# Masked products on GpSimd become block copies and column scalings in a gated delta mixer; all attention gates run on VectorE

## The chip, the cores and the metric

The kernel runs on one core of one Trainium2 chip. The metric is the device time of one execution in microseconds. A core has a matrix engine (TensorE, PE in the rows), and three engines for elementwise work: VectorE (DVE), ScalarE (ACT) and GpSimd (POOL). SyncE (SP) issues most DMAs. Each engine runs its own queue of instructions in order, and waits on semaphores for the others.

## The reference

Two model blocks are computed one after the other on 512 tokens of width 1024, all in float32. The first has two attention layers, worked in four units each; the change touches the gates of their outputs:

```python
def _merge(a_att, b_att, a_z, b_z, g_a, g_b, w_o_a, w_o_b, w_out):
    o_a = (a_att * jax.nn.silu(a_z)) @ w_o_a
    o_b = (b_att * jax.nn.silu(b_z)) @ w_o_b
    ...
```

The second block has two layers with feed-forward parts, a mixer and cross attention each. The second layer's mixer is a gated delta rule with 8 heads of width 128, in chunks of 128 tokens (4 chunks):

```python
    kkt = jnp.einsum('bhnid,bhnjd->bhnij', kb, k) * decay
    amat = jnp.eye(C, dtype=jnp.float32) + jnp.where(strict, kkt, 0.0)
    ...
    sol = lax.linalg.triangular_solve(amat, rhs, left_side=True, lower=True, unit_diagonal=True)
    ...
    def step(state, inp):
        q_i, k_i, u_i, w_i, qk_i, g_i = inp
        v_new = u_i - jnp.einsum('bhcd,bhde->bhce', w_i, state)
        o = (jnp.einsum('bhcd,bhde->bhce', q_i * jnp.exp(g_i)[..., None], state)
             + jnp.einsum('bhij,bhje->bhie', qk_i, v_new))
        ...
```

`q` and `k` are normalized by their length, `q`, `k` and `v` come from a causal convolution of four taps and a SiLU, and the result `o` is normalized over a head's columns, weighted, and multiplied with SiLU of a gate `z`.

## The kernel before

Matrix products with weights are done as three products of split operands: each weight tile `ws` is split into `wh` (ScalarE, line 114) and `wl` (VectorE, line 115), each activation into a high and a low part (`nh`, `nl` or `hh`, `hl`), and TensorE multiplies high by high, low by high and high by low (lines 131 to 133). Weights come in tiles of 512 KB by SP's queue.

In the attention layers, `gate` (line 897) multiplies a unit's finished output `o` (from L526) with the silu `z` and sends it to DRAM. There are four units in a layer; `o` has 1536 columns in the first layer and 1024 in the second. The last unit's gate (u = 3) is on VectorE, the others are on GpSimd. Around them the next unit's rotary products (L461 to L464, GpSimd), splits `hl` (L471, VectorE) and casts `qA`, `kA` (L479, VectorE) run for TensorE's transposes (L478) and scores (L493, L494).

The mixer `mixer1` (line 1733) goes through its 8 heads as a pipeline in rounds of some 41 us, one head's products entering while older heads are finished. In a head:

- `head` projects `k`, `q`, `z` and `v`, with the convolution steps `xc` (L1248, VectorE, four taps over 512 columns) and SiLUs (`kT`, `qT`, `vT`, L1488 and L1489). `e` holds the decays (L1522, L1525). `key` multiplies `e` by `rk`, the key lengths (L1543, GpSimd). `product` and `scaled` make `U` from the key products, `e` and a scale (L1550, L1554, VectorE).
- `solve` sends the 32 x 32 diagonal blocks of U to DRAM (`ud`) and fetches their 16 x 16 blocks as `D`. GpSimd inverts these by 15 steps of two instructions each, `T` (L1605) and `Y` (L1607), on 32 partitions. `Y` goes out as `yd` and back as `soC`.
- `inverse` spreads `soC` into the block-diagonal `X` (L1626, GpSimd, a product of a broadcast `soC` with the mask in `lev`). TensorE transposes X (L1635). At levels 4 and 5, GpSimd clears `W` (L1643) and makes `B`, U masked to the off-diagonal blocks of that level (L1644, a product with another mask in `lev`), which TensorE multiplies (L1648). VectorE corrects X and `Z` (L1655, L1656).
- `steps` runs the four chunks: TensorE multiplies the state (L1684, L1685), VectorE makes `R`, the new state and `o` (L1687, L1701, L1707). Then `o` is scaled by its columns of `orq` (L1722, GpSimd), and `finish` transposes it for the output (L1727, L1729).

`lev` is one tile of 128 x 384: two masks for the levels and the mask of the 16 x 16 diagonal blocks, fetched at the start of the mixer.

TensorE's order is written out by hand, by generators that yield. The other engines' instructions, and SP's DMAs, are ordered by the builder, which runs a timeline of its own and lets each engine take what is ready there first. A change of one instruction can so move others in the queues of VectorE, GpSimd and SP.

Of the kernel before, what the change touches and what calls it, by code (L numbers as in the profile page):

```python
# [8 lines left out]
F32 = mybir.dt.float32  # L9
# [3 lines left out]
OP = mybir.AluOpType  # L13
AX = mybir.AxisListType

P = 128
D = 1024
NCH = 8
S = 512
# [348 lines left out]
class Block1:  # L368
# [528 lines left out]
    def gate(self, l, u, o, z):  # L897

        n = (NT if l == 0 else 4) * 256
        eng = self.net.nc.vector if u == 3 else self.net.nc.gpsimd  # L900
        eng.tensor_tensor(out=o[:, :n], in0=o[:, :n], in1=z[:, :n], op=OP.mult)
        self.net.nc.sync.dma_start(self.units(self.od, l, u), o[:, :n])

    def early_gate(self, l, j):
# [208 lines left out]
class Block2:  # L1113
# [323 lines left out]
    def decays(self, pool):  # L1437

        net, nc, I = self.net, self.net.nc, self.net.I
        out = {}  # L1440
        yield from self.proj(I["dn_ab"], out, "p1", 16)
        yield
        ab = pool.tile([P, S], F32, name="ab", tag="dnB", bufs=1)[:16, :]
        nc.vector.tensor_tensor(ab, out["ps"], self.rb[:16, :], op=OP.mult)
        pt = net.psum("p3")
        for t in range(4):
            nc.tensor.transpose(pt[:, t * 16:(t + 1) * 16], ab[:, t * P:(t + 1) * P], net.ident[:16, :16])
        t3 = lambda name: pool.tile([P, 4, 8], F32, name=name, tag=f"dc{name}", bufs=1)
        v = pt[:, :64].rearrange("p (t a) -> p t a", a=16)
        dt = net.bcast_row(I["dn_dt_bias_2"][0], 8, "dtb", pool)  # L1450
        al = net.bcast_row(I["dn_a_log_2"][0], 8, "alog", pool)
        beta, x, gc = t3("beta"), t3("x"), t3("gc")
        nc.scalar.activation(beta, v[:, :, 8:16], AF.Tanh, scale=0.5)
        nc.vector.tensor_scalar(beta, beta, 0.5, 0.5, op0=OP.mult, op1=OP.add)
        nc.vector.tensor_tensor(x, v[:, :, 0:8], dt.unsqueeze(1).to_broadcast([P, 4, 8]), op=OP.add)
        sp = self.softplus(x.rearrange("p t h -> p (t h)"), 32, pool)
        nc.scalar.activation(al, al, AF.Exp)
        nc.vector.scalar_tensor_tensor(x, sp.rearrange("p (t h) -> p t h", h=8), -1.0,
                                       al.unsqueeze(1).to_broadcast([P, 4, 8]), op0=OP.mult, op1=OP.mult)
        yield  # L1460
        pg = net.psum("p3")
        g2 = x.rearrange("p t h -> p (t h)")
        nc.tensor.matmul(pg[:, 0:32], net.c["triu"], g2, start=True, stop=True)
        nc.tensor.matmul(pg[:, 32:64], net.c["ones"], g2, start=True, stop=True)
        nc.vector.tensor_copy(gc, pg[:, 0:32].rearrange("p (t h) -> p t h", h=8))
        gl = pg[:, 32:64].rearrange("p (t h) -> p t h", h=8)
        ngc, egc, egl, dk = t3("ngc"), t3("egc"), t3("egl"), t3("dk")
        nc.vector.tensor_scalar(ngc, gc, -1.0, None, op0=OP.mult)
        nc.scalar.activation(egc, gc, AF.Exp)
        nc.scalar.activation(egl, gl, AF.Exp)  # L1470
        nc.vector.tensor_tensor(dk, gl, gc, op=OP.subtract)
        nc.scalar.activation(dk, dk, AF.Exp)
        self.dc = dict(beta=beta, gc=gc, ngc=ngc, egc=egc, egl=egl, dk=dk)
        yield
# [16 lines left out]
    def head(self, h, hd, pool, late):  # L1491

        net, nc, I = self.net, self.net.nc, self.net.I
        cw = self.cw
        q4 = lambda a: a.rearrange("p (t d) -> p t d", d=P)
        bc = lambda a: a.unsqueeze(2).to_broadcast([P, 4, P])
        tl = lambda name, bufs: pool.tile([P, S], F32, name=name, tag=f"dn{name}", bufs=bufs)
# [6 lines left out]
        cols = lambda a: lambda t: a[:, t * P:(t + 1) * P]  # L1504
# [9 lines left out]
        dc, e, U, A = {}, tl("e", 1), tl("U", 2), tl("A", 3)  # L1514
# [21 lines left out]
        def key():  # L1536
            rk = st["k"]
            for n in ("b", "s", "w"):
                st[n] = small("n" + n)
            nc.vector.tensor_tensor(st["b"], rk, dc["beta"], op=OP.mult)  # L1540
            nc.vector.tensor_tensor(st["s"], rk, dc["dk"], op=OP.mult)
            nc.vector.scalar_tensor_tensor(st["w"], st["b"], -1.0, dc["egc"], op0=OP.mult, op1=OP.mult)
            nc.gpsimd.tensor_tensor(out=q4(e), in0=q4(e), in1=bc(rk), op=OP.mult)  # L1543

        def product(m, n):
            ps = net.psum("p3")
# [10 lines left out]
        z = tl("z", 3)  # L1557
# [58 lines left out]
    def inverse(self, hd, pool, wait):  # L1616

        net, nc = self.net, self.net.nc
        mm = nc.tensor.matmul
        q4 = lambda a: a.rearrange("p (t d) -> p t d", d=P)  # L1620
        tl = lambda name, bufs: pool.tile([P, S], F32, name=name, tag=f"dn{name}", bufs=bufs)
        lev = lambda l: self.lev[:, (l - 4) * P:(l - 3) * P].unsqueeze(1).to_broadcast([P, 4, P])
        U = hd["U"]
        hd["X"] = X = tl("X", 2)
        blocks = [P, 4, 8, 16]
        nc.gpsimd.tensor_tensor(out=X.rearrange("p (t m b) -> p t m b", t=4, b=16),  # L1626
                                in0=hd["blocks"].unsqueeze(2).to_broadcast(blocks),
                                in1=self.lev[:, 2 * P:].rearrange("p (m b) -> p m b", b=16).unsqueeze(1).to_broadcast(blocks),
                                op=OP.mult)
        Z = tl("Z", 1)  # L1630
        for _ in range(wait):
            yield
        ps = net.psum("pT")
        for t in range(4):
            nc.tensor.transpose(ps[:, t * P:(t + 1) * P], X[:, t * P:(t + 1) * P], net.ident)  # L1635
        nc.scalar.activation(Z, ps, AF.Copy)
        tiles = [slice(t * P, (t + 1) * P) for t in range(4)]
        for l in range(4, 6):
            n = 1 << l
            half = lambda a, i: a.rearrange("p (m two b) -> p m two b", two=2, b=n)[:, :, i, :]  # L1640
            dense = lambda a: a.rearrange("p (m b) -> p m b", b=n)
            B, W = tl("B", 1), tl("W", 2)
            nc.gpsimd.memset(W, 0.0)  # L1643
            nc.gpsimd.tensor_tensor(out=q4(B), in0=q4(U), in1=lev(l), op=OP.mult)  # L1644
            yield
            pw = net.psum("pT")
            for t, sl in enumerate(tiles):
                mm(dense(pw[:, t * 64:(t + 1) * 64]), B[:, sl], half(Z[:, sl], 0), start=True, stop=True)  # L1648
            nc.scalar.activation(half(W, 0), dense(pw[:, :256]), AF.Copy)
            yield  # L1650
            px = net.psum("p1")
            for t, sl in enumerate(tiles):
                mm(dense(px[:, t * 64:(t + 1) * 64]), W[:, sl], half(X[:, sl], 1), start=True, stop=True)
                mm(dense(px[:, 256 + t * 64:256 + (t + 1) * 64]), X[:, sl], half(W[:, sl], 0), start=True, stop=True)
            nc.vector.tensor_tensor(half(X, 1), half(X, 1), dense(px[:, :256]), op=OP.subtract)  # L1655
            nc.vector.tensor_tensor(half(Z, 0), half(Z, 0), dense(px[:, 256:]), op=OP.subtract)  # L1656
        yield
        h0, h1 = slice(0, HD), slice(HD, P)
        right = lambda a, t: a[:, t * P + HD:(t + 1) * P]
        pw = net.psum("pT")  # L1660
        for t in range(4):
            mm(pw[h1, t * HD:(t + 1) * HD], right(U, t)[h0], Z[h0, t * P:t * P + HD], start=True, stop=True)
        W = tl("W", 2)
        nc.scalar.activation(W[h1, :256], pw[h1, :256], AF.Copy)
        yield
        px = net.psum("p1")
        for t in range(4):
            mm(px[h0, t * HD:(t + 1) * HD], W[h1, t * HD:(t + 1) * HD], right(X, t)[h1], start=True, stop=True)
        nc.vector.tensor_scalar(q4(X)[h0, :, HD:], px[h0, :256].rearrange("p (t d) -> p t d", d=HD), -1.0, None, op0=OP.mult)

    def steps(self, h, hd, pool):

        net, nc = self.net, self.net.nc
        mm = nc.tensor.matmul
        small = lambda name, bufs=2: pool.tile([P, P], F32, name=name, tag=f"st{name}", bufs=bufs)
        q4 = lambda a: a.rearrange("p (t d) -> p t d", d=P)
        o = pool.tile([P, S], F32, name="o", tag="dno", bufs=2)
# [41 lines left out]
        nc.vector.tensor_tensor(ss, ss, rq, op=OP.mult)  # L1719
        r = net.rsqrt(ss, 4, 1.0 / P, EPS)  # L1720
        nc.vector.tensor_tensor(rq, r, rq, op=OP.mult)
        nc.gpsimd.tensor_tensor(out=q4(o), in0=q4(o), in1=rq.unsqueeze(2).to_broadcast([P, 4, P]), op=OP.mult)  # L1722

        def finish():
            ps = net.psum("p3")
# [7 lines left out]
    def mixer1(self):  # L1733
        net, nc, I = self.net, self.net.nc, self.net.I
        stats = self.norm("mix_norm_2", 1)
        with net.tc.tile_pool(name="mix1", bufs=2) as pool:
            self.lev = pool.tile([P, 3 * P], F32, name="lev", tag="lev", bufs=1)
            nc.sync.dma_start(self.lev, I["lev"])
            self.cw = pool.tile([P, 96], F32, name="cwh", tag="cwh", bufs=1)
            nc.vector.tensor_scalar(self.cw, net.col["dn_conv_w_2"], 0.5, None, op0=OP.mult)  # L1740
            hds = [{} for _ in range(8)]
# [373 lines left out]
```

## Time and profile before

| | us |
|---|---|
| median of the 3 runs shown | 3708.18 (3705.26 to 3711.72) |
| profiled execution | 3708.82 |
| its span, first to last instruction | 3707.0 |
| TensorE busy | 3613.7 (97%) |
| VectorE busy | 2060.9 (56%) |
| ScalarE busy | 1375.7 (37%) |
| GpSimd busy | 715.0 (19%) |
| mean granted clock of TensorE | 0.993 |

Busy time is the sum of an engine's instruction durations; register, branch, semaphore and DMA-issuing instructions are not in it. A timeline row has the start, the duration, the engine, the line, the operation with the tiles written and read, their shapes, and in brackets the idle time before it and what ended it. The mixer lies between about 2780 and 3200 us, the attention layers between 80 and 1260 us.

### The profile page before, as it was taken

What the parts mean: (1) busy time and instruction counts of PE and PEld (TensorE: products, weight loads), DVE (VectorE), ACT (ScalarE), POOL (GpSimd) and SP (SyncE); (2) the same over time, 40 slices, a digit from 0 to 9 for tenths busy, and PEclk for the clock granted to TensorE, in tenths of its full rate; (3) what the DMA queues carried; (4) which work ended last, traced back from release to release, by engine and by line L of the source; (5) the groups of instructions that cost most, each with busy time, mean ns of one, the idle gap of its engine ahead of it and who ended that gap; (6) DMA issues with size and microseconds to landing.
All of it is one profiled execution on the core that took longest, in us unless ns stands there. A gap on an engine that the chain in (4) does not pass through costs nothing.

```text
span 3707.0 us, 51470 instructions
## 1 busy us (share of the span) xinstructions
PE 3613.7 (97%) x19706; PEld 2992.2 (81%) x19706; DVE 2060.9 (56%) x4228; ACT 1375.7 (37%) x2407; POOL 715.0 (19%) x889
## 2 busy tenths in 40 slices
PE   8999999999999999999999999999999999999998
PEld 6887778888887778888778888888888887788887
DVE  6565773366566464334666433443347887664335
ACT  4334443234345332224654322322233333443223
POOL 1222330002233011102320100210013444101001
PEclk9999999999999999999999999999999999999999
DMA  8434113243322333333122333333333212323333
GB/s 277 121 118 136 57 50 123 63 149 90 88 69 65 139 105 97 97 94 105 57 91 64 108 97 97 97 97 97 97 98 114 57 57 74 115 77 91 103 97 103
DMA packets 135718, 364.35 MB, mean 98 GB/s; under 512 B 30000, under 2 KB 43184, under 8 KB 134960
## 3 DMA queue, kind: packets, MB, share of 16 engines
q1 hardware_dynamic: 135472, 361.06, 31.6%
q8 instruction: 155, 2.54, 0.3%
q14 instruction: 91, 0.75, 0.1%
HBM read 331.64 MB, written 19.66 MB: 95 GB/s over the span
## 4 chain that ended last, share of the span: by engine, by line
PE 88%; DVE 6%; ACT 2%; DMA 2%; issue 1%; POOL 1%; SPq 0%; DVEq 0%; ACTq 0%; POOLq 0%
PE p L131 15%; PE p L133 15%; PE p L132 15%; PE pS L131 7%; PE pS L132 7%; PE pS L133 6%; PE po L519 2%; PE pT L132 2%; PE pT L131 2%; PE pT L133 2%; PE po L132 2%; PE po L133 2%; PE po L131 2%; DVE wl L115 1%; PE pS L493 1%
## 5 line engine op out<-in xcount | busy, mean ns | idle before, releaser
L114 ACT ACTIVATE wh<-ws 128x1024 fp32r<-128x1024 f32 (+4 forms) x561 | 563.8, 1006 | 1424.2 <-PE p L132 677.4
L115 DVE TENSOR_TENSOR wl<-ws,wh 128x1024 fp32r<-128x1024 f32 (+4 forms) x561 | 662.2, 1181 | 259.7 <-ACT wh L114 257.6
L131 PE MATMUL p<-nh,wh 128*128 128x512 f32 x1084 | 429.0, 397 | 4.5 <-ACT nh L1131 2.0
L133 PE MATMUL p<-nh,wl 128*128 128x512 f32 x1084 | 424.6, 392 | 4.5 <-DVE wl L115 4.5
L132 PE MATMUL p<-nl,wh 128*128 128x512 f32 x1084 | 423.8, 391 | 1.9 <-DVE nl L115 1.9
L1198 POOL TENSOR_TENSOR g<-g,rb 128x512 f32<-128x512 f32 x88 | 149.7, 1703 | 1137.2 <-ACT g L1197 1137.2
L131 PE MATMUL pS<-nh,wh 128*128 128x512 f32 x620 | 254.1, 410 | 1.0 <-DVE xr L1181 1.0
L133 PEld LDWEIGHTS p<-nh,wl 128*128 128x128 f32 x1084 | 203.4, 188 | 50.2 <-DVE wl L115 6.0
L133 PE MATMUL pS<-nh,wl 128*128 128x512 f32 x620 | 242.5, 391 | 0.0
L132 PE MATMUL pS<-nl,wh 128*128 128x512 f32 x620 | 242.2, 391 | 0.0
L131 PEld LDWEIGHTS p<-nh,wh 128*128 128x128 f32 x1084 | 203.6, 188 | 46.7 <-ACT nh L1131 2.5
L132 PEld LDWEIGHTS p<-nl,wh 128*128 128x128 f32 x1084 | 203.4, 188 | 42.4 <-DVE nl L115 2.2
L1196 DVE TENSOR_TENSOR g<-p,rb 128x512 f32<-128x512 f32 x88 | 60.5, 691 | 227.7 <-PE p L133 217.5
L131 PE MATMUL p<-hxh,wh 128*128 128x512 f32 (+1 forms) x456 | 183.2, 402 | 0.8 <-DVE wT L502 0.8
L132 PE MATMUL p<-hl,wh 128*128 128x512 f32 (+1 forms) x488 | 179.8, 369 | 0.0
L133 PE MATMUL p<-hh,wl 128*128 128x512 f32 (+1 forms) x488 | 179.4, 368 | 0.0
L131 PE MATMUL p<-hh,wh 128*128 128x512 f32 (+1 forms) x488 | 179.3, 368 | 0.0
L133 PE MATMUL p<-hxh,wl 128*128 128x512 f32 (+1 forms) x456 | 169.9, 373 | 0.0
L132 PE MATMUL p<-hxl,wh 128*128 128x512 f32 (+1 forms) x456 | 169.8, 372 | 0.0
L1140 POOL TENSOR_TENSOR acc<-acc,sq 128x512 f32<-128x512 f32 x48 | 73.6, 1533 | 481.5 <-ACT sq L1139 479.5
L509 POOL TENSOR_SCALAR p<-p,rinv 128x768 f32<-128x768 f32 (+2 forms) x128 | 103.3, 807 | 253.8 <-DVE rinv L508 143.7
L1211 DVE SCALAR_TENSOR_TENSOR xr<-p,xr 128x512 f32<-128x512 f32 (+1 forms) x68 | 42.5, 627 | 169.6 <-PE p L133 169.5
(591 smaller groups left out, 8780.8 us busy)
## 6 DMA issues: line engine op xcount, KB each, us to landing
ws<-in_ffn_w_in_dram SPq DMA_DIRECT2D x176, 512.0 KB
ws<-in_ffn_w_out_dram SPq DMA_DIRECT2D x64, 512.0 KB
ws<-in_w_in_tok_dram SPq DMA_DIRECT2D x52, 512.0 KB
wh<-in_w_ada_dram SPq DMA_DIRECT2D x48, 512.0 KB
ws<-in_ffn_w_out_dram SPq DMA_DIRECT2D x40, 384.0 KB
ws<-in_w_out_dram SPq DMA_DIRECT2D x24, 512.0 KB
ws<-in_dn_qkv_dram SPq DMA_DIRECT2D x24, 512.0 KB
ws<-in_xa_wk_dram SPq DMA_DIRECT2D x16, 512.0 KB
```

Source lines behind the costliest of these rows:

```text
L114: self.last_hi = self.nc.scalar.activation(hi, src, AF.Copy)
L115: (eng or self.nc.vector).tensor_tensor(out=lo, in0=src, in1=hi.bitcast(F32), op=OP.subtract)
L131: mm(pt, sh, mh, start=first and i == 0, stop=False)
L132: mm(pt, sh, ml, start=False, stop=False)
L133: mm(pt, sl, mh, start=False, stop=last and i == n - 1)
L493: mm(ps, q, kA[:, k0:k1], start=True, stop=False)
L509: nc.gpsimd.tensor_scalar(p, p, r, 0.5, op0=OP.mult, op1=OP.mult)
L519: self.net.nc.tensor.matmul(ps[h:h + HD, :], v, w, start=i < 2, stop=i >= len(parts) - 2)
L1140: (nc.vector if c == 7 else nc.gpsimd).tensor_tensor(out=acc, in0=acc, in1=sq, op=OP.add)
L1196: nc.vector.tensor_tensor(t, pg, self.rb, op=OP.mult)
L1198: nc.gpsimd.tensor_tensor(out=t, in0=t, in1=self.rb, op=OP.mult)
L1211: nc.vector.scalar_tensor_tensor(x, ps, 0.5, x, op0=OP.mult, op1=OP.add)
```

## The change

All eight gates run on VectorE. In the mixer, GpSimd's products with a mask or a broadcast vector are replaced. `e` and `o` are scaled by four instructions of 128 columns, each with a pointer to one scalar per partition. `B` has one buffer for each level, cleared once at the start, and the blocks that the mask let through are copied into it: four of 16 partitions at level 4, two of 32 at level 5. X is cleared, and eight instructions of 32 partitions scale `soC` by a column of `even` (1 on the partitions of the even 16-blocks in the first, on those of the odd in the second) into the 16 columns of its block. `even` comes from two reductions of the mask on VectorE at the start of the mixer; only 64 KB of `lev` are fetched, into a buffer of the tag `dnsq`. `ab` moves from the tag `dnB` to `dnW`.

```diff
@@ gate
-        eng = self.net.nc.vector if u == 3 else self.net.nc.gpsimd
-        eng.tensor_tensor(out=o[:, :n], in0=o[:, :n], in1=z[:, :n], op=OP.mult)
+        self.net.nc.vector.tensor_tensor(out=o[:, :n], in0=o[:, :n], in1=z[:, :n], op=OP.mult)
@@ decays
-        ab = pool.tile([P, S], F32, name="ab", tag="dnB", bufs=1)[:16, :]
+        ab = pool.tile([P, S], F32, name="ab", tag="dnW", bufs=2)[:16, :]
@@ head, key
-            nc.gpsimd.tensor_tensor(out=q4(e), in0=q4(e), in1=bc(rk), op=OP.mult)
+            for t in range(4):
+                at = cols(e)(t)
+                nc.gpsimd.tensor_scalar(at, at, rk[:, t:t + 1], None, op0=OP.mult)
@@ inverse
-        lev = lambda l: self.lev[:, (l - 4) * P:(l - 3) * P].unsqueeze(1).to_broadcast([P, 4, P])
...
-        blocks = [P, 4, 8, 16]
-        nc.gpsimd.tensor_tensor(out=X.rearrange("p (t m b) -> p t m b", t=4, b=16),
-                                in0=hd["blocks"].unsqueeze(2).to_broadcast(blocks),
-                                in1=self.lev[:, 2 * P:].rearrange("p (m b) -> p m b", b=16).unsqueeze(1).to_broadcast(blocks),
-                                op=OP.mult)
+        nc.gpsimd.memset(X, 0.0)
+        for u in range(0, P, 32):
+            for i in range(2):
+                c = u + 16 * i
+                nc.gpsimd.tensor_scalar(q4(X)[u:u + 32, :, c:c + 16], hd["blocks"][u:u + 32], self.even[u:u + 32, i:i + 1], None,
+                                        op0=OP.mult)
...
-            B, W = tl("B", 1), tl("W", 2)
+            B, W = self.B[l], tl("W", 2)
             nc.gpsimd.memset(W, 0.0)
-            nc.gpsimd.tensor_tensor(out=q4(B), in0=q4(U), in1=lev(l), op=OP.mult)
+            for u in range(0, P, 2 * n):
+                at = lambda a: q4(a)[u:u + n, :, u + n:u + 2 * n]
+                nc.gpsimd.tensor_copy(at(B), at(U))
@@ steps
-        nc.gpsimd.tensor_tensor(out=q4(o), in0=q4(o), in1=rq.unsqueeze(2).to_broadcast([P, 4, P]), op=OP.mult)
+        for t in range(4):
+            at = o[:, t * P:(t + 1) * P]
+            nc.gpsimd.tensor_scalar(at, at, rq[:, t:t + 1], None, op0=OP.mult)
@@ mixer1
-            self.lev = pool.tile([P, 3 * P], F32, name="lev", tag="lev", bufs=1)
-            nc.sync.dma_start(self.lev, I["lev"])
+            self.B = {l: pool.tile([P, S], F32, name="B", tag=f"dnB{l}", bufs=1) for l in (4, 5)}
+            for b in self.B.values():
+                nc.gpsimd.memset(b, 0.0)
+            lev = pool.tile([P, P], F32, name="lev", tag="dnsq", bufs=1)
+            nc.sync.dma_start(lev, I["lev"][:, 2 * P:])
+            self.even = pool.tile([P, 2], F32, name="even", tag="even", bufs=1)
+            v = lev.rearrange("p (m two b) -> p two m b", two=2, b=16)
+            for i in range(2):
+                nc.vector.tensor_reduce(self.even[:, i:i + 1], v[:, i, :, 0], AX.X, OP.add)
```

TensorE's order is the same before and after. GpSimd's queue in one round, from the X of one head to the first solve step of the next, stood like this before (`xp` are the three columns ahead of a convolution's input):

```order
L1626 TENSOR_TENSOR X<-soC,lev 128x512
L1240 MEMSET xp 128x3 x2
L1644 TENSOR_TENSOR B<-U,lev 128x512
L1543 TENSOR_TENSOR e<-e,rk 128x512
L1644 TENSOR_TENSOR B<-U,lev 128x512
L1605 TENSOR_TENSOR T<-D,Y 32x15
```

and stands like this after:

```order
L1629 TENSOR_SCALAR X<-soC,even 32x4x16 x8
L1239 MEMSET xp 128x3 x2
L1544 TENSOR_SCALAR e<-e,rk 128x128 x4
L1625 MEMSET X 128x512
L1647 COPY B<-U 16x4x16 x4
L1647 COPY B<-U 32x4x32 x2
L1606 TENSOR_TENSOR T<-D,Y 32x15
```

The level-5 `B`, which waited for the level-4 product of TensorE and stood ahead of `e`, is now made together with level 4, behind `e`; X is cleared well ahead of its pieces.

Further on in GpSimd's round, in the middle of the solve, the scaling of `o` stood here before:

```order
L1605 TENSOR_TENSOR T<-D,Y 32x60
L1643 MEMSET W 128x512
L1607 TENSOR_TENSOR Y<-Y,T 32x6x10
L1722 TENSOR_TENSOR o<-o,orq 128x512
L1605 TENSOR_TENSOR T<-D,Y 32x55
```

and stands here after:

```order
L1644 MEMSET W 128x512
L1606 TENSOR_TENSOR T<-D,Y 32x60
L1727 TENSOR_SCALAR o<-o,orq 128x128
L1608 TENSOR_TENSOR Y<-Y,T 32x10x6
L1727 TENSOR_SCALAR o<-o,orq 128x128 x3
L1606 TENSOR_TENSOR T<-D,Y 32x63
```

The `T` of 60 columns comes twice in a solve. The scaling was behind the second, with ten solve steps left; it is now behind the first, with nineteen left.

VectorE's queue around the second product into U (L1554, the end of U) stood like this before:

```order
L1550 TENSOR_TENSOR U<-p_27040,e 128x512
L1554 TENSOR_TENSOR U<-U,p_27056 128x512
L1655 TENSOR_TENSOR X<-X,p_27108 128x16x16
L1656 TENSOR_TENSOR Z<-Z,p_27108 128x16x16
L1573 SCALAR_TENSOR_TENSOR zh<-pS,rb 128x512
L115 TENSOR_TENSOR wl<-ws,wh 128x1024
```

and stands like this after:

```order
L1658 TENSOR_TENSOR X<-X,p_27176 128x16x16
L1551 TENSOR_TENSOR U<-p_27108,e 128x512
L1659 TENSOR_TENSOR Z<-Z,p_27176 128x16x16
L1574 SCALAR_TENSOR_TENSOR zh<-pS,rb 128x512
L1555 TENSOR_TENSOR U<-U,p_27124 128x512
L115 TENSOR_TENSOR wl<-ws,wh 128x1024
```

U's second product has moved behind the corrections of X and Z and behind `zh`. In SP's queue one weight load moves between `ud` and `D`, and one between `yd` and `soC`.

## Rows read from the trace of the kernel before

**Rows 1.** The page: busy time of each engine, and one group of instructions.

```profile
PE 3613.7 (97%) x19706; PEld 2992.2 (81%) x19706; DVE 2060.9 (56%) x4228; ACT 1375.7 (37%) x2407; POOL 715.0 (19%) x889
...
L115 DVE TENSOR_TENSOR wl<-ws,wh 128x1024 fp32r<-128x1024 f32 (+4 forms) x561 | 662.2, 1181 | 259.7 <-ACT wh L114 257.6
```

**Rows 2.** TensorE's waits over the span: total us, times, longest.

```profile
PE po L1684 <- DVE o L1707: 5.4, 6, 1.1
...
PE pS L493 <- DVE qA L479: 3.5, 5, 1.2
...
PE p L1502 <- DVE vT L1489: 3.0, 5, 0.8
...
PE p L132 <- DVE nl L115: 1.9, 1, 1.9
...
PE p L478 <- DVE hl L471: 1.7, 1, 1.7
```

**Rows 3.** The gate's line: duration in ns (lowest/median/highest), first and last start, forms.

```profile
L901 POOL TENSOR_TENSOR o<-o,z x6: 2376/2950/3874, 246.4 to 1171.9; 128x1536 f32<-128x1536 f32 x3, 128x1024 f32<-128x1024 f32 x3
...
L901 DVE TENSOR_TENSOR o<-o,z x2: 1226/1492/1759, 601.2 to 1243.5; 128x1536 f32<-128x1536 f32 x1, 128x1024 f32<-128x1024 f32 x1
```

**Rows 4.** VectorE's timeline beside two gates: start, us, line, operation, [idle before].

```profile
246.56 3.36 DVE L147 TENSOR_SCALAR rb<-rv 128x8 int32<-128x8 int32 x1
...
1172.40 2.50 DVE L471 TENSOR_TENSOR hl<-qn,hl 128x256 fp32r<-128x256 f32 x2 [2.40 <-ACT hl L470]
```

**Rows 5.** GpSimd's timeline in one round of the mixer.

```profile
2956.88 1.28 POOL L1626 TENSOR_TENSOR X<-soC,lev 128x512 f32<-128x512 f32 x1 [3.91 <-DMA soC<-yd]
...
2980.09 0.23 POOL L1605 TENSOR_TENSOR T<-D,Y 32x15 f32<-32x15 f32 x1 [1.54 <-DMA D<-ud]
...
2983.43 0.31 POOL L1605 TENSOR_TENSOR T<-D,Y 32x60 f32<-32x60 f32 x1
...
2987.82 1.03 POOL L1722 TENSOR_TENSOR o<-o,orq 128x512 f32<-128x512 f32 x1
...
2988.82 1.25 POOL L1605 TENSOR_TENSOR T<-D,Y 32x55 f32<-32x55 f32 x1
...
2998.45 1.28 POOL L1626 TENSOR_TENSOR X<-soC,lev 128x512 f32<-128x512 f32 x1 [3.88 <-DMA soC<-yd]
```

**Rows 6.** VectorE's timeline in the same round.

```profile
2956.86 1.84 DVE L1248 SCALAR_TENSOR_TENSOR xc<-xp,cwh,xc 128x512 f32<-128x512 f32 x1
...
2959.23 0.74 DVE L1248 SCALAR_TENSOR_TENSOR xc<-xp,cwh,xc 128x512 f32<-128x512 f32 x1
...
2973.77 0.69 DVE L1554 TENSOR_TENSOR U<-U,p 128x512 f32<-128x512 f32 x1
...
2974.58 0.42 DVE L1655 TENSOR_TENSOR X<-X,p 128x256 f32<-128x256 f32 x1
...
2975.33 0.69 DVE L1573 SCALAR_TENSOR_TENSOR zh<-pS,rb 128x512 f32<-128x512 f32 x1
...
2987.18 0.16 DVE L1721 TENSOR_TENSOR orq<-ry,orq 128x4 f32<-128x4 f32 x1
...
2988.30 1.64 DVE L115 TENSOR_TENSOR wl<-ws,wh 128x1024 fp32r<-128x1024 f32 x1 [0.17 <-ACT wh L114]
```

**Rows 7.** TensorE's timeline in the same round and the next.

```profile
2960.48 0.49 PE L1684 MATMUL po<-state,kT 128*128 128x128 f32 x2 [1.11 <-DVE o L1707]
...
2993.92 0.55 PE L1502 MATMUL p<-c_ident,vT 128*128 128x128 f32 x3 [0.83 <-DVE vT L1489]
...
3008.32 0.60 PE L1635 MATMUL pT<-c_ident,X 128*128 128x128 f32 x4
```

**Rows 8.** GpSimd's scalings by a pointer in other stages: timeline, then line 509.

```profile
1770.72 0.61 POOL L1354 TENSOR_SCALAR dp<-dp,drin 128x128 f32<-128x128 f32 x1 [7.32 <-DVE drin L1353]
...
1773.69 0.93 POOL L1354 TENSOR_SCALAR dp<-dp,drin 128x256 f32<-128x256 f32 x1 [1.91 <-DVE drin L1353]
...
L509 POOL TENSOR_SCALAR pc<-pc,rinv x32: 472/478/1534, 176.8 to 581.5; 128x256 f32<-128x256 f32 x32
```

## The prediction

> **What bounds the kernel now.** I read the page first: TensorE is busy for 3613.7 of 3707.0 us [rows 1], so a change on GpSimd or VectorE is worth only what it moves in TensorE's 93 us of waiting. Next came TensorE's waits by cause [rows 2]: none names GpSimd. The largest that touch the changed code all name VectorE: 5.4 us for `o` at L1707, 3.0 us for `vT`, 1.9 us for `nl`, 1.7 us for `hl`, and the `qA` waits of attention. So I asked what makes VectorE late there, with the timelines of both engines side by side. The reader is to see a coincidence. While GpSimd runs a gate (median 2950 ns [rows 3]), a VectorE instruction on 8 columns takes 3.36 us and a pair of `hl` splits 2.50 us [rows 4]. While it runs the masked product into X (1.28 us [rows 5]), a convolution step `xc` takes 1.84 us where its neighbour takes 0.74 [rows 6], and TensorE then waits 1.11 us for `o` [rows 7]. The reverse is there as well: a solve step `T` of 55 columns takes 1.25 us behind VectorE's `wl` [rows 5, 6], where the step of 60 columns took 0.31 a few us earlier [rows 5]. The two engines exclude each other on some operand pairs, for a whole instruction. The change shortens single instructions of GpSimd, but lengthens its work in sum.
>
> **Gates.** Six products leave GpSimd and six join VectorE, at 1.23 us (1024 columns) or 1.76 us (1536) each [rows 3]. At 1172 VectorE had stood idle before the two `hl` splits, which then took 2.50 us; the gate now fits into that idle time and the splits shrink. Those splits feed `qA`, for which TensorE waits 1.2 us at the longest [rows 2], here: I take -1.0. At 1086.8 a gate of 2.4 us stood ahead of two rotary products in GpSimd's queue, and their result came late to `hl`, for which TensorE waited 1.7 us [rows 2]: -1.4. Elsewhere a blocked VectorE cost TensorE next to nothing: -0.1. Sum -2.5. The bounds are -5.2, all of the `hl` and `qA` waits in [rows 2], and +1.8, one gate of VectorE's that meets a late matmul. The output DMA behind each gate leaves earlier by the difference.
>
> **Masked product X, off the `xc` steps.** One instruction of 1.28 us becomes a memset ahead of its wait, and eight scalings of 32 partitions x 64 elements behind it. The wait for `o` came six times, 5.4 us in all [rows 2]. The pieces come some us later (below), so the long block goes; a short solve step may still stand in its place. I keep 0.2 us in each of five rounds: -4.3 (0 to -5.4). Of the `nl` wait of 1.9 us [rows 2], with the last head's X beside it, I take -1.0 (0 to -1.9).
>
> **Scaling of `o` and `e`.** Each product of 1.03 us becomes four column scalings. The nearest row is a scaling of 128x128 by a pointer, one operation: 0.61 us. A form with two operations takes 0.478 us for 256 columns, so about 0.38 for 128 if its start costs what the first form's does [rows 8]. I take 0.61, the same form: 2.4 us where 1.03 stood (bound 1.5). For `e` this lies ahead of the product that reads it, and VectorE comes to that later than before; I cost it at nothing. If that cover went, it would add up to 1.4 us to U. For `o` the place matters. Before, it ran at 2987.82 and delayed `wl` at 2988.30 (1.64 us, against a mean of 1.18) [rows 1, 5, 6]. From there VectorE runs nearly without a gap to `vT`, for which TensorE waits 0.83 us at 2993.92 [rows 7]. Four pieces, each getting in ahead of one of VectorE's instructions, delay that chain by up to 1.5 us where 0.5 was lost: I take +0.6 in six rounds, +3.6 (-1 to +6.6).
>
> **U, the solve and X.** This is the one chain with little slack. VectorE's order puts the second product into U behind X, Z and `zh`. It ended at 2974.46; now X starts at 2974.58, X and Z take the 0.75 that lies from there to `zh`, and U, `zh` and U take 0.69 each, less 0.08 of overlap between two: U is ready near 2977.25, 2.8 later [rows 6]. Two of SP's weight loads move past DMAs of this chain: one between `ud` and D lies in the wait for `ud`, one between `yd` and `soC` waits for a `wl` that is through by then; both at nothing. The level-4 and level-5 copies, six of some 0.3 us after U, lie in the wait for D, which left GpSimd idle for 1.54 us even behind the product that they replace [rows 5]. So the solve starts at 2980.09 + 2.8 = 2982.9. Ten steps took 3.34 us up to the `T` of 60 columns, at 2983.43 [rows 5]; with two memsets of W now ahead of it (0.5 us net) it is done at 2987.0. Here the first piece of `o` now stands, and waits for `orq`, which ends at 2987.34 [rows 6]: it is through at 2988.0. Nineteen solve steps and three pieces remain, where ten steps remained after `o` before. Those ten took from 2988.82 to 2994.5, 0.57 each beside a full VectorE, against 0.33 before it fills [rows 5]. At 0.5 the nineteen take 9.5, the pieces 1.8, and 0.7 goes to a `wl` of 1.18 us met on the way: the solve ends at 3000.0 (2997 to 3002), where it ended at 2994.5. The two DMAs behind it take 3.88 us [rows 5]: the pieces of X start at 3003.9. Each has 64 elements: 0.46 us, by the slope of the pointer form from 128 to 256 columns (0.61 to 0.93) [rows 8]; 0.31 if they cost what a small step does; 0.57 where VectorE holds them. Eight make 3.7 (2.5 to 4.6): X is there at 3007.6 (3003.4 to 3010.5). TensorE transposes it at 3008.32 [rows 7], less the 1.1 us at L1684 that goes, plus the 0.6 at `vT`: 3007.8. So the middle value is just in time and the bounds lie 4.4 below and 2.7 above. A wait that can only add is taken at 0.6 in six rounds: +3.6 (0 to +15).
>
> **Start.** Two reductions of `lev` into `even` stand in VectorE's queue ahead of `nl`, behind a DMA of 64 KB. By the 3.88 us that two small transfers in a row take [rows 5], one takes two, and most of that has passed: +0.3 (0 to +2).
>
> **Sum.** -2.5 - 4.3 - 1.0 + 3.6 + 3.6 + 0.3 = -0.3 against the profiled execution's 3708.8 us, so 3708.5; that execution lay 0.6 above the median, so 3708.
>
> On one-input instructions the Trainium skill (GPSIMD Engine Reference, 4.1 Engine selection) says that GpSimd runs them at about line rate. The two-operation row, 0.83 ns an element, agrees; the one-operation pointer row, at 2.5 ns an element, doesn't [rows 8]. By the rule the pieces of `o` and X would cost some 0.35 us, and the sum would be that of the first rival.
>
> **Rivals.** *X in time.* The pieces are short, fit between VectorE's instructions, and X keeps its slack. Then -2.5 for the gates, -5.0 at L1684, -1.5 at `nl`, +0.3 at the start and -0.5 at `vT`: -9.2, 3699 (3695 to 3704). For it: a two-input step of 60 columns on 32 partitions takes 0.31 us [rows 5]. Against it: the pointer row, and U's later place, which is certain.
>
> *The solve becomes the bound (slower).* Nineteen steps at 0.57, pieces of X at 0.57: TensorE stands at the transpose of X (L1635) for 2.2 us in six rounds, and at `vT` 1.1 us longer: -2.5 - 4.3 - 1.0 + 0.3 + 6.6 + 13.2 = +12.3, 3720 (3715 to 3725). It decides once X comes later than about 3009.5 on the clock of the round above. For it: the pace of the ten steps behind 2988.82. Against it: that TensorE's standing still would empty VectorE's queue, and steps then run at 0.33. The Trainium skill (SBUF — State Buffer, Who interferes with whom) speaks for it: the ports that both engines share are locked for a whole instruction, by GpSimd or by a VectorE instruction with two SBUF inputs. The 1.25 us step behind `wl` agrees [rows 5, 6].
>
> *Nothing moves in the mixer.* The pieces queue back to back and block as the long product did; X has room. Only the gates count: 3706 (3704 to 3709).
>
> **How the numbers follow.** Forecast 0.34 (3703 to 3714), X in time 0.32, the solve as bound 0.26, nothing in the mixer 0.08. This kernel's measurement tells about 0.2%, 7.4 us, from no change: below 3700.8 is faster, above 3715.6 slower. Of X in time 0.26 lies below, plus 0.01 of the forecast: 0.27. Of the solve 0.22 lies above, plus 0.03 of the forecast: 0.25. The same: 0.48. Cutting a tenth on either side gives 3697 to 3719.
>
> **What would show it.** The wait for `o` at L1684 falls from six times 0.9 us to under 0.3; no VectorE instruction beside X takes 1.8 us. The scalings read 0.6 us (or 0.38: first rival). The second product into U starts behind `zh`. A new wait of TensorE at L1635 for X, 0 to 1.2 us, is the forecast; over 2 us the slower rival; none, with a gap between X's last piece and its transpose of over 2 us, the first. The `vT` wait grows from 3.0 us to some 6. I am wrong altogether if `e` delays U, or if TensorE's waits outside the mixer and the gates change by more than a few us.

## The result, and the profile after

The changed kernel takes 3734.95 us (median of 6 runs, 3731.91 to 3739.99) against 3706.39 us for the kernel before in the same comparison: a ratio of 1.0077, 95% interval 1.0064 to 1.0090, so some 28 us slower. The profiled execution has a span of 3732.3 us, 25.3 over that of before. The prediction was 3708 us with a range of 3697 to 3719: wrong, and beyond the price of its own slower rival (3720), which named the mechanism.

The page of the changed kernel, busy time of each engine:

```profile
PE 3627.8 (97%) x19706; PEld 3001.2 (80%) x19706; DVE 2028.5 (54%) x4236; ACT 1375.4 (37%) x2407; POOL 758.8 (20%) x1029
```

VectorE is busy for 32 us less than before [rows 1], GpSimd for 44 us more. So GpSimd did stop holding VectorE up, and the time was lost all the same. TensorE's waits of the changed kernel, over the span (total, times, longest):

```profile
PE pT L1636 <- POOL X L1629: 18.3, 5, 4.2
...
PE p L1501 <- DVE vT L1488: 3.1, 5, 0.7
...
PE p L1732 <- POOL o L1727: 2.2, 1, 2.2
...
PE p L478 <- DVE hl L471: 1.1, 1, 1.1
...
PE p L132 <- DVE nl L115: 0.5, 1, 0.5
```

The wait of 5.4 us for `o` [rows 2] is no longer in the list, and that for `nl` fell from 1.9 to 0.5. But there is a new wait, now the longest of all, and it names GpSimd: TensorE waits for X ahead of its transpose, five times, 3.7 us on average. One such round, GpSimd's timeline first (where a row holds several instructions, its time is that of all):

```profile
2933.40 2.35 POOL L1544 TENSOR_SCALAR e<-e,rk 128x128 f32<-128x128 f32 x4 [3.52 <-DVE rk L1533]
...
2948.64 0.21 POOL L1606 TENSOR_TENSOR T<-D,Y 32x15 f32<-32x15 f32 x1 [3.77 <-DMA D<-ud]
...
2952.95 0.60 POOL L1727 TENSOR_SCALAR o<-o,orq 128x128 f32<-128x128 f32 x1
...
2954.59 2.88 POOL L1727 TENSOR_SCALAR o<-o,orq 128x128 f32<-128x128 f32 x3
...
2965.51 0.74 POOL L1608 TENSOR_TENSOR Y<-Y,T 32x15 f32<-32x15 f32 x1
2971.08 4.58 POOL L1629 TENSOR_SCALAR X<-soC,even 32x64 f32<-32x64 f32 x8 [4.83 <-DMA soC<-yd]
```

VectorE's in the same round:

```profile
2939.26 0.42 DVE L1658 TENSOR_TENSOR X<-X,p 128x256 f32<-128x256 f32 x1 [2.51 <-PE p L1657]
2939.59 0.68 DVE L1551 TENSOR_TENSOR U<-p,e 128x512 f32<-128x512 f32 x1
...
2941.12 0.67 DVE L1555 TENSOR_TENSOR U<-U,p 128x512 f32<-128x512 f32 x1
```

SP's queue in the same round, a row for each issue, and then three issues of the kernel before:

```profile
2943.68 0.38 SPq L121 DMA_DIRECT2D ws<-in_dn_qkv_dram  x1
2944.78 0.80 SPq L1600 DMA_DIRECT2D D<-ud  x2
...
2966.28 0.78 SPq L1612 DMA_DIRECT2D yd<-Y  x2
2967.10 0.42 SPq L121 DMA_DIRECT2D ws<-in_dn_qkv_dram  x1
2968.24 0.38 SPq L1614 DMA_DIRECT2D soC<-yd  x1
```

```profile
2977.53 0.95 SPq L1599 DMA_DIRECT2D D<-ud  x2
...
2994.56 0.80 SPq L1611 DMA_DIRECT2D yd<-Y  x2
2996.51 0.39 SPq L1613 DMA_DIRECT2D soC<-yd  x1
```

And TensorE's transpose of X at the end:

```profile
2975.72 1.12 PE L1636 MATMUL pT<-c_ident,X 128*128 128x128 f32 x4 [3.72 <-POOL X L1629]
```

The rounds are now 45 to 47 us long (from one such wait to the next), where they were some 41. The wait itself is not all of it. The last row shows the transposes at 1.12 us where they took 0.60 before [rows 7].

TensorE's 19706 matmuls took 3613.7 us before [rows 1] and take 3627.8 now. So 14.1 of the 25.3 us are slower matmuls, and 11.2 are more standing still: 18.3 for X and 2.2 for `o` in the last round, less 5.4 and 1.4 for the waits that went or shrank and less some smaller ones. Nearly all of it lies in five rounds, from the transpose of X at the end of the first wait to the fifth one behind it. These are the stretches of the kernel before and of the changed one (length, then busy time of TensorE, its weight loads, VectorE, ScalarE and GpSimd with instruction counts, granted clock, DMA share, GB/s):

```profile
2925.47:3135.40 209.93, 199.76 (x1241) 170.84 (x1239) 182.01 (x466) 78.37 (x152) 90.51 (x197) 0.99 0.21 60
```

```profile
2929.71:3163.32 233.61, 210.59 (x1238) 177.57 (x1239) 159.64 (x456) 78.38 (x152) 130.01 (x288) 0.94 0.19 52
```

The five rounds are 23.7 us longer. TensorE is busy in them for 10.8 us more, at a mean granted clock of 0.94 where it was 0.99, and stands still for 12.9 us more. Around two of the waits of the changed kernel:

```profile
3021.00:3025.00 4.00, 4.00 (x27) 3.61 (x28) 1.83 (x9) 2.02 (x4) 0.48 (x3) 1.00 0.01 4
3056.00:3066.00 10.00, 5.77 (x33) 4.86 (x32) 6.23 (x17) 3.02 (x6) 4.33 (x10) 0.89 0.40 116
3066.00:3070.00 4.00, 4.00 (x15) 3.42 (x14) 1.74 (x9) 1.12 (x2) 0.09 (x1) 0.50 0.00 0
```

Around the wait that ends at 3065.76 TensorE was busy for 5.77 of 10 us, and then the granted clock is 0.50, the lower of its two levels (1.2 of 2.4 GHz). It is not so behind each wait: after the one that ends at 3020.94 it stays at 1.00.

### The profile page after: what moved, and what is told of

The parts are those of the page before. It is cut to its first block, busy times and chain, and to the rows that moved or that the text cites. A ratio compares the mean times of both kernels' runs of the same rounds, so it can differ in the third digit from the quotient of the medians.

```text
span 3732.3 us, 51604 instructions
## 1 busy us (share of the span) xinstructions
PE 3627.8 (97%) x19706; PEld 3001.2 (80%) x19706; DVE 2028.5 (54%) x4236; ACT 1375.4 (37%) x2407; POOL 758.8 (20%) x1029
## 4 chain that ended last, share of the span: by engine, by line
PE 85%; DVE 4%; POOL 4%; DMA 3%; ACT 2%; issue 1%; SPq 0%; DVEq 0%; POOLq 0%; ACTq 0%
PE p L131 15%; PE p L133 15%; PE p L132 15%; PE pS L131 6%; PE pS L132 6%; PE pS L133 6%; PE po L519 2%; PE pT L132 2%; PE pT L133 2%; PE pT L131 2%; PE po L132 2%; PE po L131 2%; PE po L133 2%; PE pS L493 1%; POOL Y L1608 1%
## 5 line engine op out<-in xcount | busy, mean ns | idle before, releaser
L133 PEld LDWEIGHTS pS<-nh,wl 128*128 128x128 f32 x620 | 117.4, 189 | 25.7
```

The lines of the kernel that those rows point to most:

```text
L133: mm(pt, sl, mh, start=False, stop=last and i == n - 1)
```

## The experiments

Of twelve runs, seven take the change apart, one forces the suspected delay, one changes the form of the pieces, and three look for a better version. Each was compared with the kernel before in its own series; ratios are to that. In the expectations, theory A is that X is late by a sum of delays against one slack, the slack being the time from X's last instruction on GpSimd to its transpose on TensorE.

**Gates alone.** The kernel before with the gate's two lines of the change.

```diff
-        eng = self.net.nc.vector if u == 3 else self.net.nc.gpsimd
-        eng.tensor_tensor(out=o[:, :n], in0=o[:, :n], in1=z[:, :n], op=OP.mult)
+        self.net.nc.vector.tensor_tensor(out=o[:, :n], in0=o[:, :n], in1=z[:, :n], op=OP.mult)
```

> The kernel before with the six gates on VectorE and nothing else; the mixer's queues are those of before. Forecast of the prediction: -2.5 us against before. Rival, from the trace of the changed kernel, where TensorE's work up to 1260 us ends 1.1 us later than before: the waits that go are eaten by other stretches at the lower granted clock, 0 to +2 us.

Measured: 3702.54 us, ratio 0.9995 (0.9985 to 1.0004). The ratio puts the centre 1.9 us below before, near the forecast of -2.5, and the interval includes zero. The gates have no part in the slowdown.

**The change without e.** The changed kernel with one line back.

```diff
-            for t in range(4):
-                at = cols(e)(t)
-                nc.gpsimd.tensor_scalar(at, at, rk[:, t:t + 1], None, op0=OP.mult)
+            nc.gpsimd.tensor_tensor(out=q4(e), in0=q4(e), in1=bc(rk), op=OP.mult)
```

> The changed kernel with e scaled by one product again, as before. VectorE's order and SP's order around U are then those of before, while the pieces of o and X and the copies of B stay. Theory A (X came late by a sum: U and D 3.9 us later by the order, the solve 3.2 longer, soC 1.0 later, X's pieces 3.3 longer, against 7.6 us of slack): without the first and the soC term X is ready about 1 us ahead of its transpose, no wait there, the wait for o at L1707 stays small: 3698 to 3706. Theory B (the pieces' own time is enough): X still late by over 1 us in five rounds, 3715 to 3728.

Measured: 3696.67 us, ratio 0.9977 (0.9968 to 0.9987), a little under what was expected. With this one line the change is faster than the kernel before. Its X and the transpose behind it:

```profile
2996.92 5.43 POOL L1627 TENSOR_SCALAR X<-soC,even 32x64 f32<-32x64 f32 x8 [3.92 <-DMA soC<-yd]
```

```profile
3004.77 0.60 PE L1634 MATMUL pT<-c_ident,X 128*128 128x128 f32 x4
```

X's pieces end at 3002.35, 2.4 us ahead, though they take 5.43 us here, longer than in the changed kernel. Theory B, that the pieces' own time is enough, falls.

**e alone.** The kernel before with the same line the other way round: only `e` in pieces.

> The kernel before with e alone scaled in four pieces. The order of VectorE and SP changes as in the changed kernel; X is one product. Theory A: X is 4 to 5 us later than before, inside its 7.6 us of slack, no wait for it; the long product meets other work of VectorE: 3702 to 3709. Rival (the order alone makes the loss): a wait of 2 to 4 us at the transpose of X in five rounds, 3720 to 3735.

Measured: 3707.67 us, ratio 1.0010 (1.0001 to 1.0020). No wait for X, as its product and its transpose show:

```profile
2996.96 1.54 POOL L1628 TENSOR_TENSOR X<-soC,lev 128x512 f32<-128x512 f32 x1 [3.97 <-DMA soC<-yd]
```

```profile
3001.62 0.60 PE L1637 MATMUL pT<-c_ident,X 128*128 128x128 f32 x4
```

X is ready at 2998.50 (2996.96 + 1.54), 3.1 us ahead, where the kernel before had 8.6 us [rows 5, 7]. So the pieces of `e`, with all that the builder moves for them (U and the load ahead of D), take 5.5 us of the slack and don't exhaust it. X is one long product here, yet the wait for `o` at the state's product falls from 5.4 us to 0.9: the product now runs at another moment. Against that TensorE waits 2.6 us for `o` in the last round:

```profile
PE p L1729 <- POOL o L1724: 2.6, 1, 2.6
...
PE po L1686 <- DVE o L1709: 0.9, 1, 0.9
```

**X alone.** The kernel before with the memset and the eight scalings of the change, and `even` from its whole `lev`.

> The kernel before with X alone made from a memset and eight scalings; the queues else are those of before. Theory A: X is ready 3.3 us later, inside its slack, no wait at its transpose; the xc steps beside it are delayed by single pieces, so that the wait for o at L1707 (5.4 us in all) falls by half or more: 3702 to 3706. Rival (fine pieces lock VectorE as long as one long product): the wait for o stays at 5 us or grows, 3706 to 3711.

Measured: 3699.28 us, ratio 0.9985 (0.9976 to 0.9995), a little under what was expected. The wait for `o` at the state's product is gone entirely, not halved, since the `xc` steps run at their own length again, 809 ns at the most (lowest, median, highest), where one took 1.84 us before [rows 6]:

```profile
L1248 DVE SCALAR_TENSOR_TENSOR xc<-xp,cwh,xc x72: 732/744/809, 2785.3 to 3108.5; 128x512 f32<-128x512 f32 x72
```

X's eight pieces take 5.14 us in the round from 2995.19, where the product took 1.28 and held VectorE up. Now VectorE holds up three of the pieces: they take 0.71 to 0.99 us, the others 0.44. X is ready 2.4 us ahead of its transpose in this round, and 2.9 to 3.5 in the others, but for the last (6.6).

**X, o and B undone, one at a time.** The changed kernel with one part as before. For X the masked product comes back, for `o`:

```diff
-        for t in range(4):
-            at = o[:, t * P:(t + 1) * P]
-            nc.gpsimd.tensor_scalar(at, at, rq[:, t:t + 1], None, op0=OP.mult)
+        nc.gpsimd.tensor_tensor(out=q4(o), in0=q4(o), in1=rq.unsqueeze(2).to_broadcast([P, 4, P]), op=OP.mult)
```

> The changed kernel with X made by one masked product again; e, o and B stay as changed, and so does the late U. Theory A (a sum of delays against one slack; in the changed kernel X is 3.7 us late): the product saves about 3.3 us of the 4.6 that the pieces take, X is 0.3 to 0.8 us late, most stretches at the lower granted clock behind that wait go too: 3708 to 3718. Rival (the late U, by the order, is the cause by itself): X is still 2 us or more late, 3724 to 3735.

Measured with X undone: 3708.93 us, ratio 1.0003 (0.9994 to 1.0012). X is just in time: in the five rounds TensorE waits for it once, 0.47 us, and else X is ready 0.2 to 0.4 us ahead.

> The changed kernel with o scaled by one product again; e, X and B stay as changed. Theory A: the solve is about 2.4 us shorter, and SP's weight load no longer stands between yd and soC (1.0 us): X is 0 to 0.8 us late, 3706 to 3718. Rival (the late U by itself): 3724 to 3735.

Measured with `o` undone: 3713.79 us, ratio 1.0014 (1.0004 to 1.0023). The solve is shorter, no weight load stands between `yd` and `soC`, and X is 0.9 us late at the most:

```profile
PE pT L1636 <- POOL X L1629: 4.1, 5, 0.9
```

> The changed kernel with B made by masked products again, in one buffer; e, o and X stay as changed. Theory A: the copies lie in the wait for D and are no part of the lateness, so X stays 3 to 4 us late in five rounds: 3730 to 3740. Rival (the copies, 3.0 us for six where a product took 1.4, hold up the solve): 3712 to 3725.

Measured with B undone: 3736.85 us, ratio 1.0080 (1.0063 to 1.0097), with the changed kernel's wait:

```profile
PE pT L1637 <- POOL X L1630: 18.7, 5, 4.2
```

Undoing any of three parts, `e`, X or `o`, removes most of the loss or all of it; undoing B does nothing, since the copies lie in the wait for D. That is a sum against a threshold, as theory A has it: X was 8.6 us early before, 3.1 with `e` changed, some 2.9 with X changed, 0.9 late with both, and 3.7 late with `o` as well. The terms don't add up one for one. The pieces of `o` cost some 0.5 us with X alone (2.4 early without the pieces of `e`), and 2.8 with `e` and X, where the later solve also lets a load in ahead of `soC`.

**A late U without pieces of e.** The kernel without the pieces of `e` (3696.67 us), with U's second product made to depend on a column of `zh`, so that VectorE's queue must hold it behind. `dep` is 1, so U is the same.

```diff
-            nc.vector.tensor_tensor(U, U, ps, op=OP.mult)
+            nc.vector.tensor_scalar(dep, st["zh"][:, :1], 0.0, 1.0, op0=OP.mult, op1=OP.add)
+            nc.vector.scalar_tensor_tensor(U, U, dep, ps, op0=OP.mult, op1=OP.mult)
```

> The kernel undo_e (e scaled by one product, everything else as changed) with one edit: U's second product is made to depend on a column of zh, so VectorE can take it only behind zh; the builder puts it behind the next wl too, some 4 us later than in undo_e, and a weight load stands between yd and soC again. Theory A: in undo_e X was ready 2.4 us ahead of its transpose; it is now 2 to 4 us late in five rounds, 3715 to 3735, without a single piece of e. Rival (the pieces of e make the loss by their own time on GpSimd): no wait for X, 3696 to 3704.

Measured: 3737.33 us, ratio 1.0080 (1.0067 to 1.0094). The whole loss is back, with `e` as one product:

```profile
PE pT L1647 <- POOL X L1640: 22.0, 5, 5.4
```

```profile
2982.57 1.23 DVE L115 TENSOR_TENSOR wl<-ws,wh 128x1024 fp32r<-128x1024 f32 x1
2983.72 0.74 DVE L1557 SCALAR_TENSOR_TENSOR U<-U,dep,p 128x512 f32<-128x512 f32 x1
```

So a late U is enough for the loss, without a piece of `e`. It is no exact copy of the changed kernel: U ends 3.5 us behind the start of VectorE's X, not 2.5, and no load stands ahead of D. That the pieces' own time on GpSimd costs nothing is seen in the changed kernel's round above: they are through at 2935.75, and the first product that reads `e` starts at 2939.59, behind X. The pieces of `e` cost through what the builder moved for them.

**The same pieces in another form.** The changed kernel with a second operation in the scalings of `e`, `o` and X.

```diff
-                nc.gpsimd.tensor_scalar(at, at, rk[:, t:t + 1], None, op0=OP.mult)
+                nc.gpsimd.tensor_scalar(at, at, rk[:, t:t + 1], 1.0, op0=OP.mult, op1=OP.mult)
```

> The changed kernel with a second operation, a product with 1.0, in each scaling of e, o and X: the same pieces, the same data, another form. If the form sets the price, as in line 509 of the kernel before, a piece of 128 columns takes about 0.38 us and not 0.60, one of X 0.3 and not 0.58; the builder prices it so as well, and puts U's second product ahead of X, Z and zh again. Theory A: X is ahead of its transpose by 2 us or more, no wait there: 3692 to 3700. Rival 1 (the number of pieces is the cause): X late, 3715 to 3735. Rival 2 (the form doesn't change the price, only the order): pieces read 0.6 us, 3697 to 3703.

Measured: 3697.82 us, ratio 0.9975 (0.9965 to 0.9985). Durations (lowest, median, highest, in ns) of the pieces of X and `e` in the changed kernel:

```profile
L1629 POOL TENSOR_SCALAR X<-soC,even x64: 432/443/1809, 2843.7 to 3154.1; 32x64 f32<-32x64 f32 x64
```

```profile
L1544 POOL TENSOR_SCALAR e<-e,rk x32: 601/603/607, 2812.3 to 3118.3; 128x128 f32<-128x128 f32 x32
```

and with the second operation:

```profile
L1629 POOL TENSOR_SCALAR X<-soC,even x64: 307/318/1861, 2837.1 to 3116.1; 32x64 f32<-32x64 f32 x64
```

```profile
L1544 POOL TENSOR_SCALAR e<-e,rk x32: 371/372/374, 2806.4 to 3085.5; 128x128 f32<-128x128 f32 x32
```

One more product makes a piece of 128 columns 0.23 us cheaper. The builder's timeline prices the form in that direction too: VectorE's queue has U's second product ahead of X, Z and `zh` again. No wait for X is left: its pieces end at 2996.33 (2992.21 + 4.12), the transpose runs at 3000.39. So the number of pieces alone was not the cause. Price and order both change in this run; the run without the pieces of `e` shows that the order alone is enough to have X in time.

**Scalings on ScalarE.** The changed kernel with the pieces of `o`, `e` and X as activations, such as:

```diff
-                nc.gpsimd.tensor_scalar(at, at, rk[:, t:t + 1], None, op0=OP.mult)
+                nc.scalar.activation(at, at, AF.Copy, scale=rk[:, t:t + 1])
```

> The changed kernel with the pieces of o, e and X on ScalarE (activations with a pointer to the scale) in place of GpSimd; the memset and the copies of B stay on GpSimd, the gates on VectorE. ScalarE is 37% busy, and its activations of 128 columns take 0.26 us beside VectorE. Theory A: the solve loses 2.4 us and more, X is well ahead of its transpose, neither engine holds up the xc steps: 3688 to 3697. Rival (the pieces stand ahead of wh, vn, oq and the SiLUs in ScalarE's queue, and TensorE waits for those): 3700 to 3712.

Measured: 3738.27 us, ratio 1.0081 (1.0066 to 1.0096): a miss, and beyond the rival's price. TensorE's waits in the mixer, then ScalarE's timeline:

```profile
PE po L1694 <- ACT oq L1692: 11.2, 4, 7.3
PE po L1698 <- ACT vn L1696: 10.4, 10, 1.5
PE p L1531 <- ACT sq L1529: 9.1, 1, 9.1
PE po L1686 <- DVE o L1709: 6.6, 5, 1.4
```

```profile
2972.52 2.36 ACT L1629 ACTIVATE X<-soC,even 32x64 f32<-32x64 f32 x8 [3.59 <-DMA soC<-yd]
2974.91 1.06 ACT L114 ACTIVATE wh<-ws 128x1024 fp32r<-128x1024 f32 x1
2975.87 0.26 ACT L1696 ACTIVATE vn<-po 128x128 f32<-128x128 f32 x1
```

X's pieces stand in ScalarE's queue waiting for a DMA, 3.59 us, and `wh` and `vn` behind them wait along. The two long waits, 9.1 us for `sq` at the start of the pipeline and 7.3 for `oq` at its end, also come behind X's pieces, which wait 8.37 and 3.19 us for their DMA there. I had priced the 2.4 us of work, not the wait ahead of it.

**Two versions for speed.** The change without pieces of `e`, with the second operation in those of `o` and X; and the same with `o` as one product too.

> The kernel undo_e with the second operation in the scalings of o and X. Theory A: X was in time already, so only VectorE gains from shorter pieces, at the vT wait of 2.4 us and beside wl: 0 to 3 us under undo_e, 3693 to 3697. Rival (VectorE loses as much to more frequent short pieces): as undo_e, 3696 to 3699.

Measured: 3697.19 us, ratio 0.9972 (0.9962 to 0.9983), no clear gain over the one-operation version: with X in time the pieces' price no longer reaches TensorE.

> Gates on VectorE, B by copies, X by eight scalings with the second operation; e and o by one product each as before. The product of o costs the vT chain 0.4 us a round again, and spares it three pieces: 3693 to 3698 if pieces and product cost VectorE the same; under undo_e_two if three more pieces cost more than one product, over it if they cost less.

Measured: 3694.90 us, ratio 0.9966 (0.9952 to 0.9979): the fastest here, some 12 us under the kernel before. Its interval overlaps those of the other two versions, so what `o` as one product adds is not settled.

## Why the prediction was wrong

- **The step that failed.** It is "the middle value is just in time": X at 3007.6 (3003.4 to 3010.5) against a need of 3007.8, and so +3.6 us for all its waits. The changed kernel's round, laid over that of before at VectorE's X (2974.58 there, 2939.26 here, 35.32 apart), has X ready at 2975.66 + 35.32 = 3010.98, past the upper bound, against a need of 2975.72 - 3.72 + 35.32 = 3007.32. The waits are 18.3 us, and the lower clock behind them stood in no term. The chain itself was the right one to price: the slower rival named it, and its condition (X later than about 3009.5) was met. Its own price was too low, with 13.2 us at the transpose and nothing for the clock.
- **U.** Right: predicted 2.8 us later, ready at 2941.79 + 35.32 = 2977.11, against 2977.25.
- **SP at nothing.** Wrong twice, some 2 us in all. Neither load delayed an issue: D is issued 2.99 us behind the end of U, where it was 3.07, and `soC` 1.96 behind `yd`, where it was 1.95. But both transfers landed later. From D's issue to the first `T` it took 3.86 us (2944.78 to 2948.64) where the kernel before took 2.56, and from `soC`'s issue to X 2.84 where it took 1.94. I had asked whether the load would wait, not what it would do to the DMA behind it.
- **Pieces on the chain.** The single prices were right: 0.60 us for 128 columns, 0.44 for 64 (taken at 0.61 and 0.46). On the chain the three pieces of `o` took 2.88 and the eight of X 4.58, where I had 1.8 and 3.7: 1.1 and 0.9 us too little. Of X's pieces VectorE held up two (0.80 and 0.73), and between two pieces lie some 0.07 us that I hadn't counted. The row for pieces that are held was there, the ten solve steps that took 0.57 each; I used it for the steps and only in the bound for the pieces.
- **The clock.** Not in the sum at all: most of the 10.8 us of slower matmuls in the five rounds. The waits for X cost TensorE more than their length. The longest wait in the rows of before [rows 2] is 1.9 us; these are 3.2 to 4.2.
- **The range.** The delays of the chain were put into one term, X "just in time", taken at 0.6 us a round and measured at 3.7. Four of its steps were too small and none was much too large, and past the threshold each of them counts in full, in every round.
- **What held.** `o` at L1684: predicted -4.3, the wait of 5.4 is gone. The short pieces are enough for that, as X alone shows, and so is X's later time, as `e` alone shows. `nl`: -1.0, measured -1.4. Gates: -2.5, measured alone -1.9 with an interval that includes zero. B at nothing: confirmed, though its six copies took 3.0 us and not some 1.8. With X in time the rest comes out as the first rival had it: 3699 there, 3696.67 measured without the pieces of `e`.
- **`vT`.** I took +3.6 and the wait rose from 3.0 to 3.1 us: wrong, in the other direction. The pieces of `o` waited for VectorE (0.96 us each, on average) more than they held it up.

## What to carry to other kernels

Splitting one long GpSimd instruction into pieces does free VectorE from whole-instruction blocking, but some of the pieces then wait for VectorE in turn; price a chain of pieces at the held rate, not at the free one, and add up all delays that lead to one deadline before calling any of them hidden. Where a builder orders the queues by its own prices, look at what an edit moves in other engines' queues and in the DMA queue first: here one line for `e` decided between 8 us gained and 28 lost. And try the other forms of the same instruction before giving up on a split.

## What the runs showed of the hardware that was not expected

- On GpSimd, scaling 128 x 128 by a pointer takes 0.603 us with one operation and 0.372 with a second one added; for 32 x 64, 0.443 and 0.318.
- A product on GpSimd that held VectorE up for 1.1 us a round leaves no trace there when cut into eight pieces: then some of the pieces wait (three of eight take 0.71 to 0.99 us in the round shown of the kernel with X alone changed, the others 0.44) and the VectorE instructions beside them run at their usual length.
- A 512 KB load issued 1.1 us ahead of two 16 KB transfers went with a landing some 1.3 us later (3.86 us from issue to the first solve step, 2.56 before; 2.36 in the kernel with the late U, where no load stands there). The five rounds with a wait all show it (3.25 to 3.86 us), and so does the 32 KB transfer for `soC` behind a load of its own (2.84 to 3.40 us, against 1.88 to 2.11 before). That the load delays the transfer is argued from these, not tried by itself: no run moves a load alone.
